# Sums over partitions in float32r, rotary embedding on half heads, and a token-major last stage

## The chip, the cores and the metric

The kernel runs on one core of one Trainium2 chip. The metric is the time of one execution on the device in microseconds (us). Of the core's engines the text names TensorE (PE in the rows: matrix products; PEld: the loading of their stationary operand), VectorE (DVE), ScalarE (ACT), GpSimd (POOL) and SyncE (SP, which here only issues DMAs). A matrix product of PE writes to PSUM; DVE and ACT read it from there.

## The reference

A sequence of 256 tokens with 1024 features goes through two blocks. What is computed, cut to the parts that the change touches:

```python
# first block, two layers, each: mixer (gated linear attention / stick-breaking attention), then MLP
h = layer_norm(DEEPNORM_ALPHA * h + mix, ln_g[layer, 0], ln_b[layer, 0])
h = layer_norm(DEEPNORM_ALPHA * h + sq_relu_mlp(h, ...), ln_g[layer, 1], ln_b[layer, 1])
# layer_norm: mean and variance over the 1024 features of a token

# second block, two layers
u = rms_norm(h, attn_norm_w[i])
fq, fk, fv, f_logit, rq, rk, rv, rg = split(u @ w_in[i])
fox = forgetting_attention(fq, fk, fv, f_logit)                  # 8 heads of 64
ret = chunkwise_retention(apply_rotary(rq), apply_rotary(rk) / 8, rv)   # 8 heads of 64
ret = silu(rg) * head_group_norm(ret)
h = h + concatenate([fox, ret]) @ w_out[i]
h = h + gated_conv_ffn(rms_norm(h, ffn_norm_w[i]))
gate = sigmoid(rms_norm(h, ple_norm_w[i]) @ w_ple_gate[i])
h = h + gate * (p[i] @ w_ple_proj[i])
# after both layers
out = rms_norm(h, final_norm_w)

def apply_rotary(t, cos, sin):
    t1, t2 = t[..., :32], t[..., 32:]
    return concatenate([t1 * c - t2 * s, t1 * s + t2 * c])
```

Everything is in float32.

## The kernel before

**Layout.** Activations lie feature-major: a tile of 128 partitions by 8 chunks by 256 tokens, where chunk i holds features 128i to 128i+127. A sum over features is therefore a sum over partitions (and chunks), and PE makes it: DVE and ACT first add the chunks or their squares, then a matrix of ones multiplies the result, so that every partition gets the sum.

**Products.** A product with weights is made of three products in float32r, a format that PE streams faster than float32: `mm3` (L363 to L365) multiplies high part by high part, high by low, and low by high. The weights arrive in pieces of 512 KB through SP's DMA queue (`raw`); ACT casts each piece to its high part `wh` (L324) and DVE subtracts to get its low part `wl` (L327), three pieces ahead of PE. Activations are split in the same way (L425, L426). The small products of attention, and the sums with ones, are single float32 products (one such product shows as two records in the trace).

**Order.** The program is written for a scheduler that fixes each engine's order beforehand from priorities: an instruction's priority is its place in the source, and the casts of weights stand 150 places later (`LATER`). Each engine then works strictly in its order. Small work is put into the stream of large products by hooks: `proj(..., hooks=((k, f),))` calls `f` after the k-th of 8 steps. PSUM has four accumulators (`acc`), three tiles for projections (`up`) and one for small results (`aux`).

**What the change touches.**
- Layer norm (four times): running sums of x and of x squared, each 128 x 2 x 256 (L536, L537), then `stats` (L540 ff.): four float32 products of 256 columns with ones into `aux` (L544), mean and its square on ACT (L546, L547), variance (L549, L550), reciprocal root with one correction step (`rsqrt`, L466 to L473), and the normalized x (L555, L574, L578), split for the next products (L425, L426). With `early=True` the next layer's first products start on x before it is normalized, and `settle` (L614 ff.) corrects them, so that PE has work during the chain.
- `rms_full` (L490) and gated linear attention's `s3` (L789): one float32 product of 256 columns with ones.
- `sb` (L821 ff.): in `s2` (L871) a float32 product with the matrix `nones` of -1 (L875).
- `mix2` (L927 ff.): `stat` sums the squares per token (`tok_sum`, a column per 128 tokens), and `over` spreads the result over partitions with a diagonal matrix (`spread`, L447: DVE L453, PE L454).
- Retention, four steps j a layer, each two heads of q and k: `r1` splits the projection in high and low part and multiplies by cos; `r2` swaps the halves of the heads by products with a permutation matrix (L1002, L1003), multiplies by sin (L1005) and adds (L1006); `r3` makes the scores of two heads, each with 64 rows of the array (L1014, L1020), and multiplies them by the decay (L1022, L1023); `r4` multiplies by v (`pv`, L914, L916). `g1`, `g2`: group norm with the block matrix `bd`, two float32 products (L1039).
- The end: `ple(1)` gates feature-major: for each piece DVE multiplies the gate's projection by the norm factor (L1198), ACT applies the sigmoid (L357), DVE multiplies by the per-layer embedding (L1200) and adds h (L1201). `run` (L1204 ff.) then squares (L1270, L1272), sums with ones (L1277, L1278), takes the root, multiplies by it (L1282) and writes 1 MB out in five DMAs (L1283). The host turns the result to tokens by features.

Of the kernel before, what the change touches and what calls it, by code (L numbers as in the profile page):

```python
# [10 lines left out]
F32 = mybir.dt.float32  # L11
# [4 lines left out]
P = 128  # L16
# [45 lines left out]
def feat(v):  # L62
    return v.reshape(-1, P).T
# [4 lines left out]
for _n, _w in (  # L68
# [6 lines left out]
    + [("fin", 8)]  # L75
# [10 lines left out]
for _i, _t in enumerate((  # L86
    (("ident", P), ("ones", P), ("scan", T), ("gmask", 384)),
    (("perm", P), ("ntri", P), ("nones", P), ("cos", T), ("sin", T), ("bd", P), ("dec", 8 * T)),
# [8 lines left out]
def tables():  # L97
# [10 lines left out]
    put("perm", (i == (j ^ 32)) * 1.0)  # L108
# [16 lines left out]
    put("sin", np.concatenate([-sin, sin, -sin, sin]))  # L125
# [8 lines left out]
def arrays(inp):  # L134
# [17 lines left out]
    for l in range(2):  # L152
# [6 lines left out]
        o[f"w_rqk{l}"] = pack_pair(rq, rk)  # L159
# [8 lines left out]
        o[f"w_pp{l}"] = w.reshape(2, P, 8, P).transpose(1, 2, 0, 3).reshape(1, P, -1)  # L168
        o[f"w_pg{l}"] = pack_a(a["w_ple_gate_2"][l])
# [19 lines left out]
    put("fin", feat(a["final_norm_w_2"]))  # L189
# [20 lines left out]
class Net:  # L210
# [54 lines left out]
    for _g, _n, _w, _names in (  # L265
# [3 lines left out]
        ("gd", 3, 512, "glasq qk foxq rot pl rgr"),  # L269
# [5 lines left out]
        ("gk", 2, 256, "diag lnvar"),  # L275
# [4 lines left out]
        ("gp", 2, 256, "spread"),  # L280
# [166 lines left out]
    def spread(self, r):  # L447

        nc = self.nc
        ps = self.paux()[:, 0, :]  # L450
        d = self.t([P, 2, P], "diag")
        for c in range(2):
            nc.vector.tensor_scalar(out=d[:, c, :], in0=self.tb("ident"), scalar1=r[:, c:c + 1], scalar2=None, op0=ALU.mult)  # L453
            nc.tensor.matmul(ps[:, c * P:(c + 1) * P], self.tb("ones"), d[:, c, :], start=(c == 0), stop=True, skip_group_check=True)  # L454
        out = self.t([P, T], "spread")
        nc.scalar.copy(out, ps)
        return out

# [30 lines left out]

    def rms_full(self, acc):  # L490
        ps = self.paux()[:, 0, :]
        self.nc.tensor.matmul(ps, self.tb("ones"), acc, start=True, stop=True)
        return self.rsqrt(ps, 1.0 / D, RMS_EPS, n=T, tag="rf")


    def layer_norm(self, hold, mixes, g, b, early=True):
# [41 lines left out]
        ln = {"xc": xc, "xg": xg, "g": g, "b": b}  # L538
# [149 lines left out]
    def gla(self, x):  # L688
# [35 lines left out]
        nc.vector.tensor_tensor(out=grow[:, :, 3], in0=last[:, :, 1], in1=last[:, :, 2], op=ALU.add)  # L724

# [76 lines left out]
        for a, b in ((self.ntr, "ntri"), (self.prm, "perm")):  # L802
# [18 lines left out]
    def sb(self, ln):  # L821
# [16 lines left out]
        nt, no = self.ntr, self.tb("nones")  # L838
# [32 lines left out]
        def s2(j, i):  # L871
# [3 lines left out]
            mm(pz[:, 128:256], no, sp[:, 256:384], start=False, stop=True, skip_group_check=True)  # L875
# [51 lines left out]
    def mix2(self, l, x, acc):  # L927
# [4 lines left out]
        def stat():  # L932
            nonlocal rt
# [45 lines left out]
        rps, rots, rws, ys, rrs = {}, {}, {}, {}, {}  # L979
# [332 lines left out]
```

## Time and profile before

| | us |
|---|---|
| median of 3 runs | 1319.2 |
| lowest, highest | 1317.7, 1320.73 |
| the profiled execution | 1316.79 |
| its span on the core | 1315.0 |
| PE busy | 1291.6 (98%) |
| DVE busy | 957.9 (73%) |
| ACT busy | 761.1 (58%) |
| POOL busy | 35.2 (3%) |
| granted TensorE clock, mean | 0.998 |

The span is what the profile covers; the execution's own time is 1.8 us longer. Matmuls overlap: a record's length reaches from its start to its modelled end, so the cost of a matmul in a full stream is the distance from its start to the next one's start. PE's busy share of 98% is nearly the same in every stretch, so the other engines matter where they make PE wait, and at the end, when PE has finished.

### The profile page before, as it was taken

To read this page: it belongs to the slowest core of one execution; us is meant where nothing else is said; L and a number is where in the kernel's file an instruction comes from. 1 tells how busy PE (TensorE), PEld (TensorE's weight loads), DVE (VectorE), ACT (ScalarE), POOL (GpSimd) and SP (SyncE) were. 2 spreads that over 40 slices of the span, in tenths; PEclk is the share of its full clock that TensorE was granted. 3 is DMA by queue.
4 is the path that set the end of the run, shared out by engine and by line. 5 is a ranking of instruction groups with operands and counts; after the bars stand their busy time and mean duration, and the time that the engine had idled before them with its cause. 6 is when DMAs were issued, how large, how long until landed. Compare 5 with 4: busy or idle time off the path is not lost.

```text
span 1315.0 us, 25538 instructions
## 1 busy us (share of the span) xinstructions
PE 1291.6 (98%) x10348; PEld 1244.4 (95%) x10348; DVE 957.9 (73%) x1528; ACT 761.1 (58%) x1205; POOL 35.2 (3%) x84
## 2 busy tenths in 40 slices
PE   7999999999999999999999999999999999999996
PEld 6999999999899999999989999999989899999995
DVE  6878955559557965558878688765787869885756
ACT  6565744447786744446646665444674557554554
POOL 0000000000231000000000000000001000000000
PEclk9999999999999999999999999999999999999999
DMA  7655565554543575665654465665656446655560
GB/s 266 233 156 160 185 199 186 183 180 144 177 127 113 165 233 188 185 186 191 214 171 144 127 211 181 188 185 154 226 174 209 131 126 195 191 185 184 176 209 33
DMA packets 64727, 232.49 MB, mean 177 GB/s; under 512 B 7232, under 2 KB 7632, under 8 KB 63968
## 3 DMA queue, kind: packets, MB, share of 16 engines
q1 hardware_dynamic: 62640, 221.80, 53.7%
q10 hardware_dynamic: 1328, 6.94, 1.4%
q0 software_dynamic: 640, 2.11, 0.5%
q8 instruction: 81, 1.33, 0.4%
q14 instruction: 38, 0.31, 0.1%
HBM read 227.66 MB, written 3.16 MB: 176 GB/s over the span
## 4 chain that ended last, share of the span: by engine, by line
PE 93%; DVE 4%; DMA 1%; ACT 1%; issue 0%; SPq 0%; DVEq 0%; ACTq 0%
PE up L363 20%; PE up L364 20%; PE up L365 19%; PE acc L364 9%; PE acc L365 9%; PE acc L363 9%; DVE wl L327 1%; PE aux L914 1%; PE aux L544 1%; PE acc L1069 1%; DMA raw<-in_w_gv_dram 0%; PE aux L916 0%; PE acc L1090 0%; PE acc L1014 0%; PE acc L852 0%
## 5 line engine op out<-in xcount | busy, mean ns | idle before, releaser
L327 DVE TENSOR_TENSOR wl<-raw,wh 128x1024 fp32r<-128x1024 f32 (+2 forms) x426 | 511.1, 1205 | 269.7 <-ACT wh L324 267.7
L324 ACT CAST wh<-raw 128x1024 fp32r<-128x1024 f32 (+2 forms) x426 | 439.9, 1034 | 384.6 <-PE acc L364 143.1
L363 PE MATMUL up<-b,wh 128*128 128x256 f32 (+1 forms) x2104 | 598.7, 285 | 10.7 <-ACT b L425 6.7
L364 PE MATMUL up<-b,wh 128*128 128x256 f32 (+1 forms) x2104 | 593.6, 282 | 0.4 <-DVE b L426 0.2
L365 PE MATMUL up<-b,wl 128*128 128x256 f32 (+1 forms) x2104 | 590.1, 281 | 0.0
L363 PEld LDWEIGHTS up<-b,wh 128*128 128x128 f32 x2104 | 396.7, 189 | 20.3 <-issue 6.8
L364 PEld LDWEIGHTS up<-b,wh 128*128 128x128 f32 x2104 | 396.7, 189 | 2.2 <-DVE b L426 1.0
L365 PEld LDWEIGHTS up<-b,wl 128*128 128x128 f32 x2104 | 396.8, 189 | 0.1
L364 PE MATMUL acc<-b,wh 128*128 128x256 f32 (+1 forms) x960 | 270.5, 282 | 0.0
L365 PE MATMUL acc<-b,wl 128*128 128x256 f32 (+1 forms) x960 | 270.0, 281 | 0.0
L363 PE MATMUL acc<-b,wh 128*128 128x256 f32 (+1 forms) x960 | 269.9, 281 | 0.0
L363 PEld LDWEIGHTS acc<-b,wh 128*128 128x128 f32 x960 | 181.0, 189 | 0.1
L364 PEld LDWEIGHTS acc<-b,wh 128*128 128x128 f32 x960 | 181.0, 189 | 0.1
L365 PEld LDWEIGHTS acc<-b,wl 128*128 128x128 f32 x960 | 180.9, 188 | 0.1
L425 ACT CAST b<-ffny 128x256 fp32r<-128x256 f32 x44 | 17.9, 407 | 54.0 <-DVE ffny L1142 52.1
L363 PE MATMUL up<-wh,b 128*128 128x512 f32 x96 | 39.4, 412 | 0.2 <-ACT wh L324 0.2
L364 PE MATMUL up<-wl,b 128*128 128x512 f32 x96 | 38.0, 396 | 0.5 <-DVE wl L327 0.5
L365 PE MATMUL up<-wh,b 128*128 128x512 f32 x96 | 37.7, 395 | 0.0
L1134 DVE TENSOR_TENSOR glaS<-up,rfr 128x256 f32<-128x256 f32 x44 | 18.7, 424 | 12.3 <-PE up L365 12.2
L1138 ACT ACTIVATE ffny<-glaS,vec 128x256 f32<-128x256 f32 x44 | 26.3, 598 | 0.0
L363 PEld LDWEIGHTS up<-wh,b 128*128 128x128 f32 x96 | 18.0, 188 | 5.4 <-issue 0.7
L426 DVE TENSOR_TENSOR b<-relu,b 128x512 fp32r<-128x512 f32 x32 | 21.7, 684 | 1.4 <-ACT b L425 1.4
(245 smaller groups left out, 1163.2 us busy)
## 6 DMA issues: line engine op xcount, KB each, us to landing
raw<-in_w_fu_dram SPq DMA_DIRECT2D x88, 512.0 KB, 4.2
raw<-in_w_mu_dram SPq DMA_DIRECT2D x64, 512.0 KB, 4.4
raw<-in_w_md_dram SPq DMA_DIRECT2D x64, 512.0 KB, 4.6
raw<-in_w_fd_dram SPq DMA_DIRECT2D x32, 512.0 KB, 4.4
raw<-in_w_sqk_dram SPq DMA_DIRECT2D x16, 512.0 KB, 4.5
raw<-in_w_rqk_dram SPq DMA_DIRECT2D x16, 512.0 KB, 4.5
raw<-in_w_fqk_dram SPq DMA_DIRECT2D x16, 512.0 KB, 3.7
raw<-in_w_out_dram SPq DMA_DIRECT2D x16, 512.0 KB, 3.7
```

The costliest lines, as they stand in the source:

```text
L324: i = nc.scalar.copy(hi, r).ins
L327: i = nc.vector.tensor_tensor(out=lo, in0=r, in1=hi, op=ALU.subtract).ins
L363: mm(o, wh, xh, start=first, stop=False, skip_group_check=True)
L364: mm(o, wh, xl, start=False, stop=False, skip_group_check=True)
L365: mm(o, wl, xh, start=False, stop=last, skip_group_check=True)
L425: nc.scalar.copy(out[0][:, i, :], src)
L426: nc.vector.tensor_tensor(out=out[1][:, i, :], in0=src, in1=out[0][:, i, :], op=ALU.subtract)
L544: nc.tensor.matmul(ps[:, k, :], ones, s[k][:, i, :], start=(k == 0 and i == 0), stop=(i == 1), skip_group_check=True)
L914: self.nc.tensor.matmul(pO[r, 0, :], v[:, 0, hc], ws[i][:, 0:256], start=True, stop=False, skip_group_check=True)
L1069: mm(pls[i][:, a:b], qk[r, 0, a:a + P], qk[r, 1, 0:b - a], start=(a == 0), stop=True, skip_group_check=True)
L1134: nc.vector.tensor_tensor(out=a[:, 2:], in0=ps[:, 0, :], in1=R, op=ALU.mult)
L1138: nc.scalar.activation(y, a[:, 2:], AF.Identity, scale=self.col(f"cw{l}2", f), bias=self.col(f"cb{l}", f))
```

## The change

- `colsum` replaces the float32 products with ones. ACT copies the summed tile to float32r (high part), DVE subtracts to get the rest (low part), and two float32r products with a float32r matrix (`one`, or `bdr`) add them; 1, -1 and 1/64 are exact in float32r. It is used in layer norm's `stats` (both sums side by side, 512 columns; before it DVE adds the two halves of each sum, `lna`), in `rms_full`, `s3` and the group norm. `s2` of `sb` uses the high and low parts that it has, with `nor`.
- `mix2`: `stat` calls `rms_full`, so that the factor comes out spread; `over` makes the per-token factor; `spread` is gone.
- Rotary: the weights of q and k are packed so that first and second halves of four heads (32 rows each) lie in the two tiles of a projection (`pack_half`). `r1` is then two multiplications and two half-wide adds on DVE, and the permutation and the split are gone. `r2(m)` makes the scores of four heads at once: 16 float32 products on 32 rows each, in four row groups that write to four `acc` tiles. The hooks of the four steps are a table (`RH`), and `g1(1)` moves from 14 to 15.
- The end: `last` takes the place of `ple(1)` and of the code behind it. h is transposed on PE (16 products with the identity), the gate is projected with tokens on the partitions, the sigmoid reads PSUM with the norm factor as its scale, the square comes with a sum over the free dimension (`accum_out`), POOL raises the mean to the power -0.5, DVE and ACT scale one half each, and each 128 tokens leave in two DMAs of 256 KB on SP's and ACT's queues.

```diff
+    def colsum(self, ps, w, src, names=("sumh", "suml"), shape=None):
+        shape = shape or [P, T]
+        x = self.t(shape, names[0], F32R), self.t(shape, names[1], F32R)
+        self.nc.scalar.copy(x[0], src)
+        self.nc.vector.tensor_tensor(out=x[1], in0=src, in1=x[0], op=ALU.subtract)
+        for i in range(2):
+            self.nc.tensor.matmul(ps, w, x[i], start=(i == 0), stop=(i == 1))
...
     def rms_full(self, acc):
         ps = self.paux()[:, 0, :]
-        self.nc.tensor.matmul(ps, self.tb("ones"), acc, start=True, stop=True)
+        self.colsum(ps, self.one, acc)
         return self.rsqrt(ps, 1.0 / D, RMS_EPS, n=T, tag="rf")
...
+        sa = self.t([P, 2, T], "lna")
+        for k in range(2):
+            nc.vector.tensor_tensor(out=sa[:, k, :], in0=s[k][:, 0, :], in1=s[k][:, 1, :], op=ALU.add)
...
         def stats():
             ps = self.paux()
-            for k in range(2):
-                for i in range(2):
-                    nc.tensor.matmul(ps[:, k, :], ones, s[k][:, i, :], start=(k == 0 and i == 0), stop=(i == 1), skip_group_check=True)
+            self.colsum(ps, self.one, ln["s"], ("lnh", "lnl"), [P, 2, T])
...
-            mm(pz[:, 128:256], no, sp[:, 256:384], start=False, stop=True, skip_group_check=True)
+            for k in (sh, sl):
+                mm(pz[:, 128:256], no, k[:, 256:384], start=False, stop=(k is sl), skip_group_check=True)
...
-            hi, lo = self.t([P, 2, T], "rethi", F32R), self.t([P, 2, T], "retlo", F32R)
-            nc.scalar.copy(hi, ps)
-            nc.vector.tensor_tensor(out=lo, in0=ps, in1=hi, op=ALU.subtract)
...
-            mm(pp, self.prm, hi, start=True, stop=False)
-            mm(pp, self.prm, lo, start=False, stop=True)
-            nc.vector.tensor_tensor(out=b, in0=pp, in1=C[:, 1:2, :].to_broadcast([P, 2, T]), op=ALU.mult)
-            nc.vector.tensor_tensor(out=rot, in0=rot, in1=b, op=ALU.add)
+            nc.vector.tensor_tensor(out=b, in0=ps, in1=C[:, 1:2, :].to_broadcast([P, 2, T]), op=ALU.mult)
+            for i, op in enumerate((ALU.subtract, ALU.add)):
+                nc.vector.tensor_tensor(out=rot[:, i, :], in0=rot[:, i, :], in1=b[:, 1 - i, :], op=op)
...
+        def r2(m):
+            q, k = rots[2 * m], rots[2 * m + 1]
+            pls = [self.pacc().rearrange("p a b -> p (a b)") for _ in range(4)]
+            for c, (a, b) in enumerate(((0, 256), (256, 384))):
+                for d in range(2):
+                    for i in range(4):
+                        r = slice(32 * i, 32 * i + 32)
+                        mm(pls[i][:, a:b], k[r, d, c * P:c * P + P], q[r, d, c * P:], start=(c == 0 and d == 0), stop=(d == 1),
+                           skip_group_check=True, tile_position=(32 * i, 0))
...
-        rh = self.hooked("12 16 21 25", (r1, r2, r3, r4), 4)
+        RH = {1: [(2, r1, 0)], 2: [(2, r1, 1), (6, r2, 0)], 3: [(0, r3, 0), (2, r1, 2), (3, r4, 0), (4, r3, 1)],
+              4: [(0, r4, 1), (2, r1, 3), (5, r2, 1)], 5: [(0, r3, 2), (3, r4, 2), (4, r3, 3), (6, r4, 3)]}
...
+        def leave(c, j, a, b, ps, k):
+            g = self.t([P, b - a], "pleg")
+            self.act(g, ps, "Sigmoid", scale=rt[:, c:c + 1])
+            nc.vector.tensor_tensor(out=g, in0=g, in1=pr[:, c, a:b], op=ALU.mult)
+            nn = n[:, c, a:b]
+            nc.vector.tensor_tensor(out=nn, in0=g, in1=hT[c, j][:, a - 512 * j:b - 512 * j], op=ALU.add)
+            nc.scalar.activation(g, nn, AF.Square, accum_out=ss[:, k:k + 1])
+            nc.vector.tensor_tensor(out=y[:, c, a:b], in0=nn, in1=fb[:, a:b], op=ALU.mult)
+        def close(c, k0, k1):
+            nc.vector.tensor_reduce(out=v, in_=ss[:, k0:k1], axis=mybir.AxisListType.X, op=ALU.add)
+            nc.gpsimd.tensor_scalar(out=v, in0=v, scalar1=1.0 / D, scalar2=RMS_EPS, op0=ALU.mult, op1=ALU.add)
+            nc.gpsimd.tensor_tensor(out=R, in0=v, in1=half, op=ALU.pow)
+            for i, q in ((0, nc.sync), (1, nc.scalar)):
+                yy = y[:, c, i * 512:i * 512 + 512]
+                if i == 0:
+                    nc.vector.tensor_scalar(out=yy, in0=yy, scalar1=R, scalar2=None, op0=ALU.mult)
+                else:
+                    nc.scalar.mul(yy, yy, R)
+                q.dma_start(self.out[c * P:(c + 1) * P, i * 512:i * 512 + 512], yy)
```

Two places besides the three below, in words. In the gate of the second block's first layer, the low part `suml` stands on DVE behind the four casts of rows 9, and PE has 23 products between the sum of the high part and that of the low part. In each retention, PE's order after the second set of scores is 3 products of 512 columns, the sum of `gnh`, 2 products, the sum of `gnl`; on DVE `gnl` stands behind three decay products with these scores (L1024, L1025, L1024).

**The orders at three places.** A row of an order is line, operation, and out<-in by the program's names with their numbers; `x2` is two in a row.

DVE in the first layer norm, before. `lnsum` holds the two running sums, `rfv` the variance, `spread` the mean, `wl` the low parts of weights:

```order
L536 TENSOR_TENSOR lnsum_1065<-lnsum_1065,b_166_1058 128x512
L537 TENSOR_TENSOR lnsum_1066<-lnsum_1066,lnsq_1352 128x512
L327 TENSOR_TENSOR wl_1293<-raw_1290,wh_1292 128x1024
L327 TENSOR_TENSOR wl_1361<-raw_1358,wh_1360 128x1024
L549 TENSOR_SCALAR rfv_1415<-aux_1406 128x256
```

The same place after. `lna` are the halves added, `lnl` the low part of it:

```order
L539 TENSOR_TENSOR lnsum_1089<-lnsum_1089,b_174_1082 128x512
L540 TENSOR_TENSOR lnsum_1090<-lnsum_1090,lnsq_1376 128x512
L543 TENSOR_TENSOR lna_1380<-lnsum_1089 128x256
L543 TENSOR_TENSOR lna_1380<-lnsum_1090 128x256
L333 TENSOR_TENSOR wl_1317<-raw_1314,wh_1316 128x1024
L489 TENSOR_TENSOR lnl_1435<-lna_1380,lnh_1434 128x512
L333 TENSOR_TENSOR wl_1388<-raw_1385,wh_1387 128x1024
L553 TENSOR_SCALAR rfv_1444<-aux_1433 128x256
```

Three instructions have come in ahead of the variance, and one of the two casts stands between them.

PE at the end of the first layer's retention, before: the last product with v (L914, L916: two heads, 256 and 128 columns) in the stream of `w_rg`'s projection.

```order
L365 MATMUL up_7996<-wh_7814,b_1080_7317 128x512
L914 MATMUL aux_8124<-retw_8105,b_1128_7590 64x256
L914 MATMUL aux_8124<-retw_8109,b_1128_7590 64x256
L916 MATMUL aux_8124<-retw_8105,b_1128_7590 64x128
L916 MATMUL aux_8124<-retw_8109,b_1128_7590 64x128
L363 MATMUL up_7996<-wh_7814,b_1079_7316 128x512
```

After, the same product (now L920, L922):

```order
L920 MATMUL aux_8167<-retw_8155,b_1151_7634 64x256
L369 MATMUL up_8024<-wh_7858,b_1099_7352 128x512
L920 MATMUL aux_8167<-retw_8158,b_1151_7634 64x256
L922 MATMUL aux_8167<-retw_8155,b_1151_7634 64x128
L370 MATMUL up_8024<-wl_7859,b_1099_7352 128x512
L371 MATMUL up_8024<-wh_7858,b_1100_7353 128x512
L922 MATMUL aux_8167<-retw_8158,b_1151_7634 64x128
```

The four products of the head pair no longer stand together; large products stand between them.

ACT at the end of the program, before. `rfa`, `rfr` are steps of the reciprocal root, `b` here the output:

```order
L357 ACTIVATE pleg_15557<-pleg_15557 128x256
L351 ACT_TABLE_LOAD
L1275 ACTIVATE b_2295_15615<-b_2274_15366,vec 128x256
L357 ACTIVATE rfa_15650<-rfv_15648 128x256
L357 ACTIVATE rfr_15651<-rfa_15650 128x256
```

After. `finss` are the sums of squares, `finr` the root; the first L1263 and its DMA belong to tokens 0 to 127, the second to tokens 128 to 255:

```order
L363 ACTIVATE pleg_15615<-up_15590,rsr_15484 128x256
L1263 ACTIVATE b_2293_15438<-b_2293_15438,finr_15581 128x512
L1264 DMA out_dram<-b_2293_15438 128x512
L1249 ACTIVATE pleg_15615,finss_15439<-b_2292_15437 128x256
L363 ACTIVATE pleg_15646<-up_15621,rsr_15484 128x256
L1249 ACTIVATE pleg_15646,finss_15439<-b_2292_15437 128x256
L1263 ACTIVATE b_2293_15438<-b_2293_15438,finr_15652 128x512
L1264 DMA out_dram<-b_2293_15438 128x512
```

The last two squares now stand behind the scaling of the first 128 tokens, and the root is no longer on ACT.

## Rows read from the trace of the kernel before

**Rows 1.** The page, parts 1 and 4: busy engines, and the chain's shares.

```profile
PE 1291.6 (98%) x10348; PEld 1244.4 (95%) x10348; DVE 957.9 (73%) x1528; ACT 761.1 (58%) x1205; POOL 35.2 (3%) x84
...
PE 93%; DVE 4%; DMA 1%; ACT 1%; issue 0%; SPq 0%; DVEq 0%; ACTq 0%
```

**Rows 2.** Waits of PE: tile, line, what it waited for: total, times, longest.

```profile
PE up L363 <- DVE pleg L1198: 2.8, 2, 1.6
...
PE up L363 <- ACT b L582: 1.2, 1, 1.2
...
PE aux L454 <- DVE diag L453: 0.4, 1, 0.4
```

**Rows 3.** Timeline of PE, first layer norm: start, duration, engine, line, operation.

```profile
122.49 1.99 PE L544 MATMUL aux<-lnsum,tab 128*128 128x256 f32 x8 [0.32 <-DVE lnsum L536]
124.13 0.47 PE L363 MATMUL acc<-b,wh 128*128 128x258 f32 x1
```

**Rows 4.** Timeline of PE, retention of the first layer: permutation, then scores.

```profile
657.44 0.39 PE L1002 MATMUL aux<-rethi,prm 128*128 128x512 f32 x1
657.66 0.40 PE L1003 MATMUL aux<-retlo,prm 128*128 128x512 f32 x1
...
660.12 0.70 PE L1014 MATMUL acc<-rot 64*128 64x256 f32 x4
...
660.97 0.39 PE L363 MATMUL up<-b,wh 128*128 128x256 f32 x1
```

**Rows 5.** Lines of PE by form: count, busy, mean ns (two records a product).

```profile
L875 PE MATMUL acc<-sbsp,tab 128*128 128x128 f32 x32 | 6.1, 273 | 0.0
...
L1039 PE MATMUL aux<-retsq,tab 128*128 128x256 f32 x16 | 4.1, 378 | 0.0
```

**Rows 6.** Timeline of PE: a split product with v; later, six transposes.

```profile
405.81 0.95 PE L914 MATMUL aux<-sbw,b 128*64 128x256 f32 x3
...
406.61 0.38 PE L914 MATMUL aux<-sbw,b 128*64 128x256 f32 x1
...
407.13 0.38 PE L363 MATMUL up<-b,wh 128*128 128x256 f32 x1
...
715.44 0.82 PE L1090 MATMUL acc<-tab,foxl 128*128 128x128 f32 x6
```

**Rows 7.** Timelines of DVE and of PE from the first layer norm on.

```profile
122.36 0.68 DVE L537 TENSOR_TENSOR lnsum<-lnsum,lnsq 128x512 f32<-128x512 f32 x1
122.96 2.35 DVE L327 TENSOR_TENSOR wl<-raw,wh 128x1024 fp32r<-128x1024 f32 x2
125.23 0.41 DVE L549 TENSOR_SCALAR rfv<-aux 128x256 f32<-128x256 f32 x1
...
135.46 0.69 DVE L426 TENSOR_TENSOR b<-b,b 128x512 fp32r<-128x512 f32 x1
...
137.34 0.28 PE L363 MATMUL up<-b,wh 128*128 128x256 f32 x1
```

**Rows 8.** Windows around the third layer norm: PE, PEld, DVE, ACT, POOL busy us.

```profile
425.00:450.00 25.00, 25.00 (x206) 24.79 (x205) 25.00 (x41) 19.06 (x38) 0.00 (x0) 1.00 0.43 139
```

**Rows 9.** Timeline of DVE, gate of the first layer: casts, then the norm's variance.

```profile
942.37 4.62 DVE L327 TENSOR_TENSOR wl<-raw,wh 128x1024 fp32r<-128x1024 f32 x4
946.91 0.41 DVE L466 TENSOR_SCALAR rfv<-aux 128x256 f32<-128x256 f32 x1
```

**Rows 10.** Timeline of all engines, the end of the program.

```profile
1302.59 0.28 PE L365 MATMUL up<-b,wl 128*128 128x256 f32 x1
...
1302.90 0.42 DVE L1198 TENSOR_TENSOR pleg<-up,rfr 128x256 f32<-128x256 f32 x1 [0.18 <-PE up L365]
...
1308.73 2.57 DVE L1282 TENSOR_TENSOR b<-b,rfr 128x256 f32<-128x256 f32 x5
```

**Rows 11.** Lines of POOL by form: its cheapest computing groups.

```profile
L923 POOL TENSOR_SCALAR_AFFINE_SELECT sbsp<-sbsp 128x128 f32<-128x128 f32 x32 | 8.2, 293 | 346.5 <-DVE sbsp L864 346.5
...
L1294 POOL MEMSET const-float32-0.0<- 128x1 f32 x1 | 0.1, 98 | 0.3 <-issue 0.3
```

More of the change, by code (lines that the diff above doesn't have):

```diff
@@ L87 @@
     (("ident", P), ("ones", P), ("scan", T), ("gmask", 384)),
-    (("perm", P), ("ntri", P), ("nones", P), ("cos", T), ("sin", T), ("bd", P), ("dec", 8 * T)),
+    (("ntri", P), ("nones", P), ("cos", T), ("sin", T), ("bd", P), ("dec", 8 * T)),
 )):
@@ L268 @@
         ("gc", 2, 512, "glaG sbw rethi ph"),
-        ("gd", 3, 512, "glasq qk foxq rot pl rgr"),
+        ("gd", 3, 512, "lna lnh lnl gnh gnl glasq qk foxq rot pl rgr"),
         ("ge", 1, 512, "retb ptin"),
@@ L279 @@
         ("gr", 2, 256, "rfr"),
-        ("gp", 2, 256, "spread"),
+        ("gp", 2, 256, "spread suml"),
         ("gq", 1, 512, "retc glagrow"),
@@ L445, in tok_sum @@
                                   start=(c0 + c == 0), stop=True, skip_group_check=True)
[L447 to L457, printed above, removed]
     def rsqrt(self, src, scale, eps, n=2, tag="rs"):
@@ L724, in gla @@
         nc.vector.tensor_tensor(out=grow[:, :, 3], in0=last[:, :, 1], in1=last[:, :, 2], op=ALU.add)
+        nc.scalar.copy(self.one, self.tb("ones"))
         v = self.b8().rearrange("p a b -> p (a b)").rearrange("p (c n) -> p c n", c=2)
@@ L788, in s3 @@
             pst = self.paux()[:, 0, :]
-            mm(pst, self.tb("ones"), sq[:, 0, :], start=True, stop=True)
+            self.colsum(pst, self.one, sq[:, 0, :])
             rs[j] = self.rsqrt(pst, 1.0 / 256.0, RMS_EPS, n=T, tag="rf")
@@ L801, in gla @@
             gps[j] = self.proj("w_gqk", j, x, hooks=hooks(j))
-        for a, b in ((self.ntr, "ntri"), (self.prm, "perm")):
+        for a, b in ((self.ntr, "ntri"), (self.nor, "nones"), (self.bdr, "bd")):
             i = nc.scalar.copy(a, self.tb(b)).ins
@@ L837, in sb @@
         mm = nc.tensor.matmul
-        nt, no = self.ntr, self.tb("nones")
+        nt, no = self.ntr, self.nor
         zs, sps, ws = {}, {}, {}
@@ L932, in stat, with over @@
         def stat():
+            nonlocal R
+            R = self.rms_full(acc)
+        def over():
             nonlocal rt
@@ L1037, in g2 @@
             pst = self.paux()
-            for i in range(2):
-                mm(pst[:, i, :], self.tb("bd"), rrs[c][:, i, :], start=(i == 0), stop=True, skip_group_check=True)
+            self.colsum(pst, self.bdr, rrs[c], ("gnh", "gnl"), [P, 2, T])
             pr = self.rsqrt(pst, 1.0, GN_EPS, n=2 * T, tag="rg")
@@ L1215, in run @@
         nc.scalar.dma_start(self.tab[0], A["tab0"])
-        self.ntr = self.const.tile([P, P], F32R, name="ntr")
-        self.prm = self.const.tile([P, P], F32R, name="prm")
+        self.ntr, self.nor, self.bdr, self.one = (self.const.tile([P, P], F32R, name=n) for n in ("ntr", "nor", "bdr", "one"))
         self.eps = self.const.tile([P, 1], F32, name="eps")
@@ L1261, in run @@
             x, acc = self.rms(h, f"pn{l}")
+            if l == 1:
+                return self.last(h, x, acc)
             h = self.ple(l, h, x, acc)
```

130 lines of the change are left out of this document (78 added, 52 removed).

## The prediction

> **What bounds the kernel now.** The page's busy shares come first: PE is busy 98% of the span, and in the chain of work that ended last PE holds 93% and DVE 4% [rows 1]. So a microsecond of PE's stream is a microsecond of time, and the work of DVE and ACT counts only where PE waits for it. The waits of PE say where that is: after the start, only the gate (two waits on L1198, 2.8 us together), the last layer norm (L582, 1.2 us) and the spread (0.4 us) cost anything [rows 2]. A busy share can deceive, because PE's cover is thin: in the windows around the third layer norm DVE too is busy 25.00 of 25 us [rows 8]. Third, the end: the last large product starts at 1302.59, the last multiplication ends at 1308.73 + 2.57 = 1311.3 [rows 10], so 8.7 us belong to a serial chain on DVE and ACT with PE idle, and then 3.7 us to the last transfer.
>
> **Prices.** A float32 product of 256 columns costs PE (124.13 - 122.49) / 4 = 0.41 us [rows 3], one of 128 half of it, 0.2 us. A float32r product of 512 columns costs 657.66 - 657.44 = 0.22 us [rows 4], one of 256 half, 0.11 us.
>
> **Sums.** A layer norm's four float32 products (1.64 us) become two of float32r (0.44 us): 1.2 us less, 4.8 us for four, with the first one's wait of 0.3 us [rows 3] 5.1 us. The seven single products in `s3` and `rms_full` go from 0.41 to 2 x 0.11: 7 x 0.19 = 1.3 us. The group norms' 16 records are 8 products [rows 5], 3.3 us against 4 x 0.44 = 1.8: 1.5 us. `nones` has 16 products at 0.2 us [rows 5]; two float32r products of 128 columns cost 0.06 each if they halve again, and 0.11 each if they do not: between a gain of 1.4 us and none (a small loss at 0.11, 0.3 us). I take 0.7 us, since the step from 512 to 256 does halve elsewhere. The spread loses two products of 128 columns and gets two of 256 in float32r, 0.2 us each layer. Together **-9.0 us** on PE.
>
> **Rotary.** The permutation goes: eight times 0.44 us [rows 4], 3.5 us. Its copy, subtraction and PSUM reads leave ACT and DVE, which were beside PE's work, and are worth nothing more. The scores: a pair of heads takes 660.97 - 660.12 = 0.85 us [rows 4], eight times, 6.8 us. Of the 0.85 the products explain only 0.41 + 0.2 = 0.61, for one head: the two heads, on 64 rows each, ran side by side, and 0.24 us go for entering and leaving. A set of four heads now needs two passes (first and second halves), 2 x 0.61 + 0.24 = 1.46 us if four row groups run side by side as two do; four sets, 5.8 us. Saved 1.0 us, together **-4.5 us**. That two run side by side is in the rows; that four do is not. The Trainium skill, TensorEngine Tiling (Array Packing), Key Properties, says that tiles of the array load weights and multiply independently, and its table gives up to four times for 32 rows; by it nothing would change in the sum.
>
> **What the new order costs PE.** A product with v that other products cut took 407.13 - 405.81 = 1.32 us [rows 6] where a whole one of the same sizes takes 0.85 [rows 4]: 0.47 us for each further entry. The order after has eight entries more: two at the end of each retention, one beside each layer's first forgetting attention, one in stick-breaking attention, one in gated linear attention. **+3.8 us**, between 0 (no entry costs what the one row shows) and 4.5. In each retention the sum of `gnl` comes about 5 x 0.22 + 0.2 = 1.3 us behind the scores on PE; DVE first has three products with these scores (about 0.35 us apart) and its own subtraction of 0.7, which with 0.2 us to start is 1.95. PE waits 0.6 us a layer, **+1.2 us** (0 to 2).
>
> **What the layer norms give back.** Ahead of the sums DVE now has two adds (0.41 us each as recorded, 0.35 apart) and a subtraction (0.68, 0.6 apart), and ACT a copy of 0.6 us. In the first layer norm the variance (125.23) followed right behind two casts [rows 7]; both casts still stand ahead of it, so 0.35 + 0.35 + 0.6 = 1.3 us of DVE are added before it, and nothing is taken away. Everything behind it on DVE moves by as much: the first chunk's low part ends at 135.46 + 0.69 + 1.3 = 137.4. PE wants it at 137.34 [rows 7] less the 1.2 and 0.3 us that it has saved: 135.8. A wait of 1.6 us takes the place of a slack of 1.2. The third is built alike, with DVE full [rows 8]: 1.3. The second has half a microsecond more slack: 0.3. The last one has no slack, PE waited 1.2 us already [rows 2]; PE comes 1.2 earlier and the chain ends about 1.1 later: 2.3. Together **+5.5 us**, between 0 (the scheduler's casts slide behind the chain and cost nobody) and 8 (DVE's four times 1.3 on top of PE's 5.1, less slack).
>
> **Gate of the first layer.** `suml` waits behind four casts, until 946.9 [rows 9]; PE, with 23 products in hand, waits some 1.7 us there. The factor is then as late as before (it was read at 946.91 [rows 9]), but PE's later waits, 1.4 for the gate and 0.6 at the spread [rows 2], mostly go, since PE is then as late as they are. **-0.5 us**, from +1.5 to -1.5.
>
> **The end.** PE gets 16 transposes at about 0.11 us (six within 0.82 us, of which 0.28 is the last one's length [rows 6]), 1.8 us, and loses the second wait for the gate, 1.4 us [rows 2], as the sigmoid reads PSUM itself; the per-token sum may wait 0.2. **+0.6 us**. Behind the last product the chain is: sigmoid, multiplication, addition, square, 0.45 us each with the step to the next engine; 0.3 to start; 0.4 for reading the accumulator and adding three numbers; POOL; 0.65 for the scale; and 0.3 because the sigmoid stands behind the square of the piece before. That is 3.45 us and POOL. POOL has run no power here. Its cheapest groups take 0.1 us (memset of one column) and 0.29 (128 columns) [rows 11]; two instructions are 0.2 to 0.6, and 2 us if a power is slow. The nearest is the second, with the steps between engines 0.75. So 4.2 us instead of 8.7, **-4.5 us**. A slower POOL counts twice, as the first 128 tokens' scale stands ahead of DVE's and ACT's last pieces: at 2 us only 2.0 us would be gained; at 0.2, 5.2. The last transfer, 256 KB as before, keeps its 3.7 us. The Trainium skill, GPSIMD Engine Reference, section 4.1, advises VectorE for elementwise work and calls GpSimd about two times slower with two inputs; no row shows that here, and the sum does not use it.
>
> **The sum.** -9.0 - 4.5 + 3.8 + 1.2 + 5.5 - 0.5 + 0.6 - 4.5 = -7.4 us. From the profiled execution, 1316.8, that gives 1309.4; that execution lies 2.4 us under the median, and from the median of 1319.2 it is **1311.8 us**.
>
> **Rivals.**
> 1. *The chains hide.* If DVE's casts slide and neither the layer norms nor `gnl` make PE wait, the 6.7 us stay gained: 1305.1. For it: only four waits of note stand in the trace [rows 2], so the order of before hid such chains well. Against: DVE is full just there [rows 8].
> 2. *Small waits eat it.* The layer norms cost 8, the gate +1.5, POOL 2 us: 2.5 + 2.0 + 2.5 = 7.0 worse, 1318.8, no change. For it: DVE's queue holds casts ahead of every new subtraction, and PE stands behind each. Against: these are three bounds at once; one or two of them give 1314 to 1316.
> 3. *Row groups of 32 do not run side by side.* One after the other, the 16 products of a set take 8 x 0.41 + 8 x 0.2 + 0.24 = 5.1 us, four sets 20.5 instead of 5.8: 14.7 worse, 1326.5, slower than before. If only two run together it is 4 x 0.61 + 0.24 = 2.7 a set, 4.9 worse, 1316.7. It decides from less than about two side by side. Against it: the pair of 64 rows [rows 4].
> 4. *The order after doesn't hold its promise on PE*, a wait of PE for four free accumulators before the scores: 1 us a set at most, inside the range.
>
> **How the numbers follow.** Forecast 0.55 (1308 to 1316), the first rival 0.2, the second 0.15 (of which 0.08 beyond 1316.5), the third 0.06 (0.05 one after the other, 0.01 in pairs), others 0.04. About 0.2%, 2.6 us, is what a measurement of this kernel can tell from no change. Faster than 1316.6: 0.55 + 0.2 + 0.07 = 0.82. Within: 0.11. Slower: 0.07. A range from 1304 to 1317.5 leaves out rival 3, the rest of rival 2 and a little below.
>
> **What would show it.** In the profile of the changed kernel: layer norm sums of 0.44 us in PE's timeline, and waits of PE at `lnl`, at the first product on normalized x, at `gnl` and `suml` with 0.5 to 2 us each; a set of scores within 1.5 us; no wait for `pleg`; the last multiplication about 4.2 us after the last product's start, with POOL's two instructions under 0.8 us. I am wrong if those waits are missing (then nearer 1305), if the sets take 2.7 or 5 us, or if POOL takes over 1 us.

## The result and the profile after

The changed kernel takes 1326.7 us (median of 6 runs, 1325.2 to 1330.0), the kernel before beside it 1319.0 (1317.7 to 1320.9): a ratio of 1.0059, 95% interval 1.0044 to 1.0074. It is slower by 0.6%, where 1311.8 us was forecast. The profiled execution took 1325.2 us, its span 1323.5.

The page's busy line and its chain, against [rows 1]: no engine has more to do by more than 1.6 us. The chain's shares can't be set against those of before: it could be followed back only for a little over half of the span, and there PE holds 47 of 53 parts. So the reason has to come from PE's waits.

```profile
PE 1292.3 (98%) x10278; PEld 1236.1 (93%) x10278; DVE 958.8 (72%) x1545; ACT 762.7 (58%) x1212; POOL 36.7 (3%) x89
...
PE 47%; DVE 3%; DMA 2%; ACT 1%; issue 0%; POOL 0%; POOLq 0%; DVEq 0%; ACTq 0%
```

PE's waits after, against [rows 2] (tile, line, what it waited for: total, times, longest). L369 to L371 are now the lines of `mm3`, L431 and L432 the split, L491 the products of `colsum`, L586 and L587 the last layer norm's normalized x, L450 `tok_sum`:

```profile
PE up L370 <- DVE pl L432: 4.2, 1, 4.2
PE up L370 <- DVE b L587: 2.4, 1, 2.4
PE up L370 <- DVE b L432: 2.0, 4, 0.7
PE up L369 <- ACT b L586: 1.8, 1, 1.8
PE aux L491 <- DVE gnl L489: 1.5, 2, 0.8
PE aux L450 <- DVE ssum L604: 1.4, 1, 1.4
PE aux L491 <- DVE suml L489: 1.1, 1, 1.1
PE aux L491 <- ACT erk L625: 0.6, 1, 0.6
...
PE up L369 <- DVE pleg L1208: 0.4, 1, 0.4
```

The longest is one that the prediction doesn't have: 4.2 us for `pl`. That is the low part of the per-layer embedding's input for the second block's first layer, on whose projection PE works while the last layer norm's chain runs. Two traces can be lined up by landmarks, the moments at which PE has begun the same amount of its products with weights. By them the kernel after is 2.0 us behind at 600 us of the trace before, ahead of that norm, and 12.8 behind at 640; 12.3 at 720, in the first layer's forgetting attention; 11.9 at 1067; 13.0 at the last large product (1315.62 for 1302.59, [rows 10]); and 8.5 at the end, since the new last stage gives 4.5 back. So nearly 11 of the 13 us lie in one stretch of 40 us around the last layer norm.

That stretch in windows (PE, PEld, DVE, ACT, POOL busy us, then PE's granted clock), before:

```profile
600.00:640.00 40.00, 38.81 (x301) 37.41 (x301) 33.48 (x61) 27.40 (x47) 0.00 (x0) 1.00 0.56 187
```

after, with single microseconds of it:

```profile
600.00:640.00 40.00, 31.41 (x200) 29.00 (x199) 30.79 (x56) 22.44 (x42) 0.00 (x0) 0.87 0.48 165
612.00:613.00 1.00, 0.58 (x3) 0.58 (x4) 0.37 (x1) 0.41 (x1) 0.00 (x0) 0.75 0.37 137
613.00:614.00 1.00, 1.00 (x6) 1.00 (x6) 0.00 (x0) 0.00 (x0) 0.00 (x0) 0.50 0.35 84
...
635.00:636.00 1.00, 1.00 (x7) 1.00 (x7) 1.00 (x4) 0.02 (x1) 0.00 (x0) 0.50 0.00 0
```

PE is busy 7.4 us less, and the mean granted clock is 0.87: it is 0.50, which is the 1.2 GHz level, from 612.4 to 616.0 us, right behind the wait for `pl`, and from 629.6 to 636.4, beginning within the second of the two waits for x. PE's timeline (start, duration, idle time before and its releaser) shows both, the products 0.21 us apart instead of 0.12:

```profile
612.42 0.54 PE L370 MATMUL up<-pl,wh 128*128 128x256 f32 x1 [4.16 <-DVE pl L432]
612.76 0.42 PE L371 MATMUL up<-ph,wl 128*128 128x256 f32 x1
612.97 0.41 PE L369 MATMUL up<-ph,wh 128*128 128x256 f32 x1
...
615.94 0.28 PE L369 MATMUL up<-ph,wh 128*128 128x256 f32 x1
...
628.02 0.50 PE L369 MATMUL up<-b,wh 128*128 128x256 f32 x2 [1.84 <-ACT b L586]
630.88 0.58 PE L370 MATMUL up<-b,wh 128*128 128x256 f32 x1 [2.36 <-DVE b L587]
631.26 0.41 PE L371 MATMUL up<-b,wl 128*128 128x256 f32 x1
631.48 0.41 PE L369 MATMUL up<-b,wh 128*128 128x256 f32 x1
```

DVE's timeline tells why `pl` was late:

```profile
610.41 0.68 DVE L540 TENSOR_TENSOR lnsum<-lnsum,lnsq 128x512 f32<-128x512 f32 x1
611.01 0.75 DVE L543 TENSOR_TENSOR lna<-lnsum 128x256 f32<-128x256 f32 x2
611.68 0.69 DVE L432 TENSOR_TENSOR pl<-ptin,ph 128x512 fp32r<-128x512 f32 x1
...
619.72 0.69 DVE L489 TENSOR_TENSOR lnl<-lna,lnh 128x512 fp32r<-128x512 f32 x1 [0.68 <-PE up L370]
620.45 0.69 DVE L432 TENSOR_TENSOR pl<-ptin,ph 128x512 fp32r<-128x512 f32 x1
621.06 1.22 DVE L333 TENSOR_TENSOR wl<-raw,wh 128x1024 fp32r<-128x1024 f32 x1
622.20 0.42 DVE L553 TENSOR_SCALAR rfv<-aux 128x256 f32<-128x256 f32 x1
```

`pl` stands right behind the adds `lna`, although its high part `ph` was cast at 407.3 us; in the kernel before, `pl` was made at 407.8. A table in the kernel lets tiles share rings of buffers, and the change put `lna`, `lnh` and `lnl` into the ring of three buffers that `pl` uses, so `pl` now gets its buffer in turn with them. And `lnl` waits until PE has read `pl` (0.68 us as shown, but 8 us behind the adds), so the norm's second sum stands behind the products with `pl`, and the normalized x behind that. From the end of the last running sum to the first low part of x it took 11.7 us before (609.1 to 620.8) and 19.7 us after (611.1 to 630.8).

### The profile page after: what moved, and what is told of

It is laid out like the page before. It is cut to its first block, busy times and chain, and to the rows that moved or that the text cites. A ratio compares the mean times of both kernels' runs of the same rounds, so it can differ in the third digit from the quotient of the medians.

```text
span 1323.5 us, 25425 instructions
## 1 busy us (share of the span) xinstructions
PE 1292.3 (98%) x10278; PEld 1236.1 (93%) x10278; DVE 958.8 (72%) x1545; ACT 762.7 (58%) x1212; POOL 36.7 (3%) x89
## 4 chain that ended last, share of the span: by engine, by line
PE 47%; DVE 3%; DMA 2%; ACT 1%; issue 0%; POOL 0%; POOLq 0%; DVEq 0%; ACTq 0%
PE up L369 12%; PE up L370 12%; PE up L371 12%; PE acc L369 3%; PE acc L370 3%; PE acc L371 3%; DMA raw<-in_w_pg_dram 1%; DVE wl L333 1%; PE aux L920 1%; ACT wh L330 1%; DMA raw<-in_w_rg_dram 1%; PE acc L1072 1%; PE acc L1093 0%; PE aux L922 0%; DVE ssum L604 0%
## 5 line engine op out<-in xcount | busy, mean ns | idle before, releaser
L369 PE MATMUL up<-b,wh 128*128 128x256 f32 x2040 | 579.7, 284 | 8.7 <-ACT b L431 6.5
L370 PE MATMUL up<-b,wh 128*128 128x256 f32 x2040 | 576.5, 283 | 4.6 <-DVE b L587 2.4
L371 PE MATMUL up<-b,wl 128*128 128x256 f32 x2040 | 576.1, 283 | 0.0
L369 PEld LDWEIGHTS up<-b,wh 128*128 128x128 f32 x2040 | 386.8, 190 | 16.3 <-ACT b L431 6.5
L370 PEld LDWEIGHTS up<-b,wh 128*128 128x128 f32 x2040 | 386.4, 189 | 7.8 <-DVE b L432 3.5
L371 PEld LDWEIGHTS up<-b,wl 128*128 128x128 f32 x2040 | 385.9, 189 | 0.2 <-DVE wl L333 0.2
L371 PE MATMUL acc<-b,wl 128*128 128x256 f32 (+1 forms) x960 | 270.0, 281 | 0.0
L369 PE MATMUL acc<-b,wh 128*128 128x256 f32 (+1 forms) x960 | 269.5, 281 | 0.0
L371 PEld LDWEIGHTS acc<-b,wl 128*128 128x128 f32 x960 | 181.3, 189 | 0.2
L369 PEld LDWEIGHTS acc<-b,wh 128*128 128x128 f32 x960 | 180.9, 188 | 0.1
L369 PE MATMUL up<-wh,b 128*128 128x512 f32 (+1 forms) x136 | 53.3, 393 | 0.2 <-ACT wh L330 0.2
L370 PE MATMUL up<-wl,b 128*128 128x512 f32 (+1 forms) x136 | 52.2, 384 | 0.5 <-DVE wl L333 0.5
L371 PE MATMUL up<-wh,b 128*128 128x512 f32 (+1 forms) x136 | 51.8, 381 | 0.0
L431 ACT CAST b<-ffny 128x256 fp32r<-128x256 f32 x44 | 17.9, 407 | 51.7 <-DVE ffny L1145 50.4
L369 PEld LDWEIGHTS up<-wh,b 128*128 128x128 f32 x136 | 25.5, 188 | 6.8 <-issue 1.5
L370 PEld LDWEIGHTS up<-wl,b 128*128 128x128 f32 x136 | 25.6, 188 | 6.4 <-issue 1.1
L371 PEld LDWEIGHTS up<-wh,b 128*128 128x128 f32 x136 | 25.6, 188 | 5.4 <-DVE erz L626 0.3
L1137 DVE TENSOR_TENSOR glaS<-up,rfr 128x256 f32<-128x256 f32 x44 | 18.7, 425 | 12.5 <-PE up L371 12.5
```

The costliest lines, as they stand in the source:

```text
L369: mm(o, wh, xh, start=first, stop=False, skip_group_check=True)
L370: mm(o, wh, xl, start=False, stop=False, skip_group_check=True)
L371: mm(o, wl, xh, start=False, stop=last, skip_group_check=True)
L431: nc.scalar.copy(out[0][:, i, :], src)
L1137: nc.vector.tensor_tensor(out=a[:, 2:], in0=ps[:, 0, :], in1=R, op=ALU.mult)
```

## Experiments

Where an experiment is compared with another on a different chip, the ratios to the kernel before beside it are used; a thousandth is 1.3 us. The landmarks compare one profiled execution with one other, stretch by stretch.

**e1: `pl` in another ring.**

```diff
-        ("gd", 3, 512, "lna lnh lnl gnh gnl glasq qk foxq rot pl rgr"),
+        ("gd", 3, 512, "lna lnh lnl gnh gnl glasq qk foxq rot rgr"),
...
-        ("gg", 2, 512, "rety erz sbl"),
+        ("gg", 2, 512, "rety erz sbl pl"),
```

> The changed kernel, with one line of its buffer table altered: the tile `pl` (low part of the per-layer embedding's input) leaves the ring `gd`, which it shares with layer norm's new `lna`, `lnh`, `lnl`, and goes into the ring `gg`. DVE can then make it 150 us before it is needed, as in the kernel before. Theory A (PE's 4.2 us wait for `pl`, the fall of the granted clock behind it, and `lnl` waiting for `pl`'s buffer, are what the prediction missed): the wait is gone (-4.3), the 9.6 us at half clock are gone (-4.3), the wait for normalized x is shorter (-2): about 1316 us (1314 to 1318). Theory B (the last layer norm's chain would keep PE waiting as long, and the clock low, whatever `pl` does): 1322 or more.

Measured: 1320.7 us, ratio 1.0009 (0.9998 to 1.0020). One name in one table gives back 6.0 us by the medians, 6.6 by the ratios; `pl` is made at 468.6 and PE does not wait for it. By the landmarks the whole of it, 6.7 us, lies in the stretch around the last layer norm. But 1320.7 is not the 1316 of theory A: the last layer norm's own waits stay, and half a clock behind them, from 625 to 632:

```profile
PE up L369 <- ACT b L586: 2.1, 1, 2.1
PE up L370 <- DVE b L432: 2.0, 4, 0.6
PE aux L450 <- DVE ssum L604: 1.8, 1, 1.8
PE up L370 <- DVE b L587: 1.8, 1, 1.8
```

```profile
625.00:632.00 7.00, 6.02 (x28) 6.03 (x29) 6.74 (x17) 4.31 (x9) 0.00 (x0) 0.51 0.34 115
```

**e10: `lnl` in another ring, `pl` left late.** The other half of the sharing: `lnl` moves from `gd` to `gg`.

> The kernel after, with the low part of the layer norm's sums (lnl) taken from the ring of two buffers gg; pl, the low part of the per-layer embedding's input, stays in gd and so stays behind lna in DVE's order. It tells two halves of the last layer norm's cost apart. If the wait of PE for pl is the dear part: it stays at about 4 us with its half clock behind it, and the time stays above 1323. If the dear part is that lnl must wait until PE has read pl's buffer (0.68 us, and the products behind it), the chain behind the sums gets some 2 us shorter and the time falls to 1322 or lower. With pl early (e1_pl_early) it was 1320.7.

Measured: 1322.6 us, ratio 1.0020 (1.0009 to 1.0032), between the two forecasts. The wait for `pl` stays as it was, with half a clock for 3.5 us behind it, but the waits for x are short and the clock behind them is full:

```profile
PE up L370 <- DVE pl L432: 4.2, 1, 4.2
...
PE up L370 <- DVE b L587: 1.2, 1, 1.2
...
PE up L369 <- ACT b L586: 0.4, 1, 0.4
```

```profile
614.00:615.00 1.00, 0.44 (x2) 0.44 (x3) 0.92 (x2) 0.55 (x1) 0.00 (x0) 0.62 0.56 209
...
629.00:637.00 8.00, 7.44 (x62) 7.44 (x63) 8.00 (x22) 7.22 (x17) 0.00 (x0) 1.00 0.38 154
```

So the ring costs in two places, and in each through a wait with a slow clock behind it: to free `pl` gives 6.6 us by the ratios, to free `lnl` 5.1. A reading of the two traces, not tested by itself, is that with `lnl` free the wait for `pl` gives the chain its time, and that with `pl` free there is no such pause and PE arrives at x before the chain does. Both moves together were not run, so the two gains can't be added.

**e3: layer norm's sums as before.** e1 with the four float32 products, without `lna`, `lnh`, `lnl`.

```diff
-            self.colsum(ps, self.one, ln["s"], ("lnh", "lnl"), [P, 2, T])
+            for k in range(2):
+                for i in range(2):
+                    nc.tensor.matmul(ps[:, k, :], ones, s[k][:, i, :], start=(k == 0 and i == 0), stop=(i == 1), skip_group_check=True)
```

> As e1, but layer norm's sums are made as before, by four float32 products, without `lna`, `lnh`, `lnl`. The prediction's step: the new sums gain 5.1 us on PE and give back 5.5 in the chains, so this one is equal to e1 within 1.5 us. Rival 1 of the prediction (the chains hide): 4 to 5 us slower than e1. A chain dearer than foreseen: 2 to 4 us faster than e1.

Measured: 1315.3 us, ratio 0.9965 (0.9951 to 0.9978). The new sums, meant to save 5.1 us of PE, cost 5.4 us net even with `pl` out of the way. The wait at the last norm is 1.2 us, as in [rows 2], and no half clock follows it.

**e6: old sums in the last layer norm alone.** The same edit under `if not early`, which holds for that norm only.

> As e1 (1320.7), but the last layer norm alone makes its sums by four float32 products; the first three keep the new ones. Theory C (e3's gain of 5.4 sits at the last layer norm: its wait of 3.9 instead of 1.2 us, and the half clock behind it): 1315.3 to 1316.5. Theory D (each of the four costs the same, 1.35): 1319.3. In between if the third, whose stretch grew by 2 us in the trace, costs its part: 1317.5.

Measured: 1316.5 us, ratio 0.9983 (0.9971 to 0.9994). That is 3.4 us faster than e1 by the ratios, where e3 is 5.8 faster; by the landmarks e6 gains 4.4 us on e1 at the last layer norm and nothing ahead of it. So most of what the new sums cost lies there, and 1 to 2.4 us in the other three together.

**e7: work in the wait.** e1 with 16 products of 512 columns that nobody reads, placed ahead of the products with the normalized x.

```diff
+        d = self.paux().rearrange("p a b -> p (a b)")
+        for _ in range(16):
+            nc.tensor.matmul(d, self.one, px[0].rearrange("p a b -> p (a b)"), start=True, stop=True, skip_group_check=True)
```

> As e1, with 16 products of 512 columns added that nobody reads, in PE's order where it waits for the last layer norm (3.7 us of work in a wait of 4.5). They add work and shorten no chain. Theory A (half of that wait's cost is the half clock behind it, 3.2 us in e1's trace): the clock stays, 1317.5 us. If the clock plays no part: 1320.7 or a little more.

Measured: 1318.1 us, ratio 0.9996 (0.9987 to 1.0005). Of the waits for x 0.3 us is left, and the stretch that ran at 0.50 in e1 is at full clock:

```profile
620.00:625.00 5.00, 4.71 (x22) 3.69 (x20) 4.90 (x13) 3.82 (x9) 0.00 (x0) 1.00 0.93 365
625.00:632.00 7.00, 6.96 (x58) 6.97 (x59) 7.00 (x19) 5.30 (x12) 0.00 (x0) 1.00 0.27 80
```

More work on the engine that sets the time, and 1.7 us less of it by the ratios, 2.6 by the medians. The two ratios' intervals overlap a little, so the times alone don't show it; by the landmarks e7 gains 2.7 us on e1 between 620 and 636 us, where the clock differs, and the mean granted clock was 0.994 to 0.996 in all eleven executions of e1, 0.996 to 0.999 in those of e7. The lost clock is thus a cost of its own, beside the wait.

**e2: `pl` late in the kernel before.** An order without a semaphore holds `pl` behind the last running sum.

```diff
+            i = nc.vector.tensor_tensor(out=px[1], in0=pt, in1=px[0], op=ALU.subtract).ins
+            self.tc.add_manual_dep(i, self.lastsum.name, mybir.DependencyInfo(mybir.DependencyClass.NoSync, mybir.DependencyReason.DATA), reason="late")
```

> The kernel before, with only an order added: the subtraction that makes `pl` stands behind the last running sum of the last layer norm on DVE. Theory A: PE waits about 4 us for it, the wait of 1.2 us for normalized x goes, and the granted clock falls: 1322 to 1326 us. Theory B (the place of `pl` matters only together with the new chain): at most 1320.

Measured: 1321.0 us, ratio 1.0013 (1.0001 to 1.0025), by neither theory's numbers. In its trace PE never waits for `pl`: the scheduler, which sees this order, put PE's products with it further back. It did not reproduce the case, and says nothing on the price of a late `pl`.

**e4 and e5: the other parts alone, on the kernel before.** e4 takes over the token-major end (`last`, the packing of its weights), e5 the rotary part (`pack_half`, `r1`, `r2`, `RH`, `g1` at 15); of e5's core:

```diff
-            mm(pp, self.prm, hi, start=True, stop=False)
-            mm(pp, self.prm, lo, start=False, stop=True)
...
+            for i, op in enumerate((ALU.subtract, ALU.add)):
+                nc.vector.tensor_tensor(out=rot[:, i, :], in0=rot[:, i, :], in1=b[:, 1 - i, :], op=op)
```

> The kernel before with the token-major end alone (`last`, its packed weights, output by tokens). The prediction's terms: +0.6 us on PE, -4.5 behind the last product: 1315 us (1313.5 to 1317). If the per-token sum makes PE wait 1.4 us as in the changed kernel's trace: 1316. If the gain hung on other parts of the change: 1318 or more.

Measured: 1316.3 us, ratio 0.9980 (0.9970 to 0.9990).

> The kernel before with the rotary part alone (half heads, scores of four heads at once, the hooks' table). The prediction's terms: permutation -3.5, scores -1.0 (the changed kernel's trace says -1.5), four further entries at the ends of the two retentions +1.9: about 1316 us (1315 to 1317.5). If the four row groups did not run side by side: 1330. If retention's new hooks made PE wait on DVE: 1318 or more.

Measured: 1316.8 us, ratio 0.9979 (0.9971 to 0.9988). Both parts are gains of over 2 us each. In e4 PE waits 1.7 us for the per-token sum:

```profile
PE aux L444 <- DVE ssum L600: 1.7, 1, 1.7
```

**e9: no products inside the split ones.** In e3, the last `r4` of a retention is hooked one step later. In the trace this joins more than the products with v of the retentions (four further entries gone): those of each first forgetting attention (`foxw`, two) and the transposes ahead of them (`foxl`, four) stand whole again too.

```diff
-              4: [(0, r4, 1), (2, r1, 3), (5, r2, 1)], 5: [(0, r3, 2), (3, r4, 2), (4, r3, 3), (6, r4, 3)]}
+              4: [(0, r4, 1), (2, r1, 3), (5, r2, 1)], 5: [(0, r3, 2), (3, r4, 2), (4, r3, 3), (7, r4, 3)]}
```

> e3_old_ln_sums with one number changed: the last step of the retention, r4 of the fourth pair, is hooked behind step 7 of the projection instead of step 6. By the order that stands for this kernel, the products with v of every retention then follow one another on PE with nothing between them, as in the kernel before. Theory: the entries that the change added cost PE 3.3 us (products with v 27.8 us against 24.5 in the kernel before, in the traces), so the time falls from 1315.3 to between 1312 and 1313. Rival: an entry costs nothing net, because what a cut lengthens on PE is slack that a later wait would take; then 1314.5 to 1316.

Measured: 1309.0 us, ratio 0.9930 (0.9916 to 0.9943), 4.6 us better than e3 by the ratios, more than either expected. Single executions of one kernel differ by stretches of half clock that come and go (last section), so the medians of few executions are a soft measure; the fastest of each, 1311.3 and 1308.6, differ by 2.7 us. By the landmarks PE gains 1.7 us in the first retention with its forgetting attention and 1.8 in the second, 3.5 together for ten entries. Ahead of the gate of the first layer 1.6 of it is taken back, as PE waits there for low parts of x (1.1 us in two waits that e3 doesn't have). So the rival holds in part, and how much of the gain in time is the cut stays open.

**e8 and e11: a repaired kernel.** e8 is e3 with e9's edit, the per-token sum hooked behind step 11 instead of 3, and one float32 product for the sum in the first layer's gate (`suml` gone). e11 is e8 with the group norm's sums in float32 too:

```diff
-            self.colsum(pst, self.bdr, rrs[c], ("gnh", "gnl"), [P, 2, T])
+            for i in range(2):
+                mm(pst[:, i, :], self.tb("bd"), rrs[c][:, i, :], start=(i == 0), stop=True, skip_group_check=True)
```

> e3 (1315.3) with three repairs of what the traces show as waits or cuts: the last product with v of each retention one step later (hook 6 to 7), so that no product with v is cut (eight entries of about 0.43 us, with those beside forgetting attention: -2.6); the per-token sum of the end at hook 11 instead of 3 (-1.1); the gate's sum in the second block's first layer as one float32 product (its wait of 1.1 for `suml` goes, 0.2 more on PE: -0.9). About 1311 us (1309 to 1313.5). If cuts cost nothing: 1313.5.

Measured: 1308.7 us, ratio 0.9924 (0.9912 to 0.9937).

> e8_repaired with the group norm's sums as two float32 products each, as in the kernel before; the group norm's low part and PE's wait for it (1.5 us in the two retentions of e8) go, and PE gets 8 products of 0.41 us for 8 of 0.22, 1.6 us more. Theory: the two cancel, 1308.7 give or take 0.7. Rival: the wait of 1.5 us was slack that a later wait takes, and the time is 1.6 us longer, 1310.3.

Measured: 1306.5 us, ratio 0.9908 (0.9894 to 0.9922). Both beat both kernels; e11 is 12.3 us faster than the kernel before, and 20.2 than the one after. Against e8 the intervals overlap, and by the landmarks e11 gains only 0.4 us in the two retentions, so that the float32 sums are better is not shown; that they are no worse is enough to say that the pair gained nothing there. Between 600 and 640 us e11 reads like the kernel before:

```profile
600.00:640.00 40.00, 38.81 (x283) 36.37 (x282) 35.16 (x66) 27.59 (x49) 0.00 (x0) 1.00 0.60 202
```

## Why the prediction was wrong, by its steps

**The step that failed is the last layer norm's.** "The last one has no slack ...: 2.3" was worked out from DVE's instructions alone, two adds and a subtraction. With `pl` out of the ring its waits come out: in e1 PE waits 2.1 + 1.8 = 3.9 us, where the step says 1.2 + 2.3 = 3.5. Two things were missing.
- *The ring.* `lna` and `lnl` were costed as time on DVE, not as buffers. Sharing put `pl` behind `lna`, and `lnl` behind PE's reading of `pl`. Price by e1: 6.0 us (4.2 of waiting, and 1.6 of clock: from 612.42 to 615.94 us PE begins 16 products in 3.5 us, which at 0.12 us each take 1.9). The order of the changed kernel has this row; the prediction looked there for casts and compared the places where its own terms lay.
- *The clock.* No term of the sum had one, and in the trace of before no wait of PE in mid-stream, of 1.6 us at most [rows 2], lowers the clock. Behind waits of 1.8 and 2.4 us the products stood at 0.21 us from 630.88 to 636.5, 26 of them in 5.6 us instead of 3.1, about 2.5 us lost; e7 shows the like.
The Trainium skill, TensorE: Matmul & The Clock Gate, HAM oscillation, tells of a kernel whose waits between groups of matmuls bring the clock to half again and again; this trace agrees, with 0.50 behind both waits. It bore on the one term of the sum that ends in waits of this length; behind the changed kernel's other waits in mid-stream, of 1.4 us and less, the clock stayed full.

**The other layer norms** were mis-sized too. With what they save on PE the sum has the first even, the second 0.9 us faster and the third 0.1 slower. By the landmarks the first is even (waits of 0.3 and 0.7 us), the second gives nothing, and the third loses 1.8: PE waits 0.6 for an `erk` on ACT ahead of the sum and 1.1 for low parts of x. By e3 and e6 the three together lose 1 to 2.4.

**Retention.** Two row groups of 64 became four of 32 and do run side by side, as the sum had it (start, duration; the next product):

```profile
676.14 1.59 PE L1014 MATMUL acc<-rot,rot 32*128 32x256 f32 x32
677.66 0.39 PE L369 MATMUL up<-b,wh 128*128 128x256 f32 x1
```

One set is 1.52 us for four heads, forecast 1.46, where two heads took 0.85 [rows 4]. The third rival's 1326.5 us, close to the result, is thus a coincidence: its mechanism is not in the trace. The waits for `gnl`, 0.75 us a layer, were forecast as 0.6. The cuts were in the sum as 3.8 us for eight entries at 0.47; e9 takes out six of these and four among the transposes, which the sum didn't have, and gains 3.5 us of PE's stream, 0.35 for an entry. So there were more entries, each at less than forecast. The group norm's 1.5 us of gain did not come: by e11, undoing it is no loss. Rotary alone, forecast at -4.5 with four of the eight entries, 1.9, is -2.6; e5 has -2.2.

**Gate of the first layer.** The waits for `suml`, 1.1, and the gate behind it, 0.4, are 1.5 us where 2.0 stood, 0.5 less as forecast. (The 2.0 are 1.6 and 0.4 in [rows 2], not the 1.4 and 0.6 of the prediction, and the second wait on L1198 is 1.2, not 1.4.) By the landmarks next to nothing of it arrives: 12.5 us behind at 940, 12.4 at 980.

**The end.** The chain behind the last product, 4.2 us forecast, is 4.3 (start, duration):

```profile
1315.62 0.28 PE L371 MATMUL up<-wh,b 128*128 128x256 f32 x1
...
1316.16 0.46 ACT L363 ACTIVATE pleg<-up,rsr 128x256 f32<-128x256 f32 x1
...
1318.35 0.19 POOL L1256 TENSOR_SCALAR finv<-finv 128x1 f32<-128x1 f32 x1 [4.02 <-DVE finv L1255]
1318.62 0.55 POOL L1257 TENSOR_TENSOR finr<-finv,finh 128x1 f32<-128x1 f32 x1
1319.21 0.72 ACT L1263 ACTIVATE b<-b,finr 128x512 f32<-128x512 f32 x1 [1.14 <-POOL finr L1257]
```

POOL's two instructions take 0.19 and 0.55 us, together under the 0.8 of the forecast, and the scale ends at 1319.93. In front of it "the per-token sum may wait 0.2" was mis-sized: 1.4 us, as DVE's sums of squares were not done at the third hook. So the part is worth 2.7 us alone (e4), not 3.9; hooked eight steps later it does not wait.

**What is left.** Between the profiled executions the sum is 15.8 us off (1309.4 for 1325.2). The ring's 5.8 (4.2 and 1.6), the clock behind x, 2.5, the waits for x, 0.7, the second and third norms, 2.6, and the per-token sum, 1.2, make 12.8. The landmarks spread the remaining 3.0 over parts that each come out short of the sum: gated linear attention (0.7), stick-breaking attention (0.5; the 0.7 for `nones` did not come), the two retentions (0.6 and 0.4) and the gate with the spread behind it (0.8). No run splits these further.

## What to carry to other kernels

A new tile is a buffer before it is work: when it joins a shared ring, list what else takes its turn there, and look where the scheduler now puts those tiles, above all the ones that feed the products which cover a chain. Trading products on the busy engine for a copy and a subtraction on others pays only where nobody waits at the end of the chain: 1.2 us of PE saved in the last layer norm cost 5 us or more in waits and clock behind it. And a wait of the matrix engine is dearer than its length, since the products behind it may run at half speed; filling it with idle products can be worth it, here about 2 us.

## What the runs showed of the hardware

- The granted clock falls to 0.50 behind waits of PE and stays there while PE streams products without a pause: 3.5 us behind 4.2 us of waiting, 5.5 us of products behind 1.8 and 2.4 with two products between. It stayed full behind 1.2 us in the kernel before and in e3, and behind 1.6 us at the first layer's gate in the kernel before.
- The same wait may or may not bring it about. Behind PE's wait for the per-token sum the clock is at half in e10 (1.5 us), e6 (1.7) and e9 (1.9), and full in e4 (1.7) and e1 (1.8). In the profiled execution of e9, 1313.3 us, there is one more such stretch at 16 to 20 us, which six of the thirteen traces have. Four of e9's other five executions took 1308.6 to 1309.0. The row behind e9's wait:

```profile
1283.00:1287.00 4.00, 4.00 (x18) 3.32 (x17) 2.34 (x6) 2.63 (x4) 0.00 (x0) 0.57 0.00 0
```

- Sixteen products of 512 columns with no reader kept the clock at 1.00 in a stretch that was at 0.50 without them (e7).
- A set of 16 float32 products on 32 rows each, in four row groups, takes 1.52 us. POOL's power on one column takes 0.55 us, its multiplication and addition 0.19.
